# Recurrence on one core: where 48 modulation steps are issued, and two heads' blocks side by side

## The chip, the cores and the metric

The kernel runs on one core of a Trainium2 chip, in one launch. The metric is the device time of that core in microseconds (us). The engines named below are PE (TensorE, the matrix multiplies), DVE (VectorE), ACT (ScalarE), POOL (GpSimd) and SP (SyncE, which here only issues transfers). Each engine runs its own list of instructions in the order in which they stand there. Before the change three runs took 1282.65, 1286.14 and 1279.99 us, with a median of 1282.65 us.

## The reference

A trunk of two layers works on 512 positions of width 1024. Layer 0 is a gated linear recurrence (8 heads of 128) with a SwiGLU feed-forward (FFN, inner width 2816). From its result one K and one V are projected. Layer 1 is a banded attention over them (16 heads of 64), with its own FFN. Every sub-layer normalises, then scales and shifts by vectors that come from a conditioning vector `c`:

```python
c_act = jax.nn.silu(c)
for layer in range(DEPTH):
    mod = c_act @ mod_w[layer] + mod_b[layer]
    sh1, sc1, g1, sh2, sc2, g2 = jnp.split(mod, N_MOD, axis=-1)
    u = modulate(rms_norm(h, norm_mix[layer]), sh1, sc1)
    mix = hgrn2_mixer(...) if layer < N_A_LAYERS else chunk_band_attention(...)
    h = h + g1[:, None, :] * mix
    u = modulate(rms_norm(h, norm_ffn[layer]), sh2, sc2)
    h = h + g2[:, None, :] * swiglu(u, ffn_w_in[layer], ffn_w_out[layer])
    if layer == N_A_LAYERS - 1:
        k_pad, v_pad = shared_kv(h, c_act, kv_norm, kv_mod_w, kv_mod_b, kv_w)
return rms_norm(h, final_norm)
```

`shared_kv` has a shift and a scale of its own from `c`. So there are 14 modulation vectors of 1024 entries. In the recurrence, position t takes from position s of the same head the value `q_t * decay(s..t) * k_s`, and `decay` is a product of the forget gates between them.

## The kernel before

**Modulation steps.** Two of the 14 vectors are made at the start; the other 12 come from `mod_vector` (line 308 on), eight steps for each vector. One step loads 128 rows of 1024 weights (512 KB) into a tile `mw` by SP (line 313) and multiplies it by the row `crow` with a sum along the row, on DVE (line 315). `mw` has two buffers, so a third load waits until the first step is done. After eight steps one small addition (line 317) gives the vector. `mod_vectors` chains vectors, and each `next(side, None)` asks for one more step. A step is held back behind the instruction that `state["mods_after"]` names when the step is asked for (line 314).

**Order.** Apart from the first part (written in a manual order), a scheduler sorts the instructions of each engine. It may take a step that the program asks for late and put it earlier, as far as its data and line 314 let it. The order that it made is fixed when the program runs: an instruction that waits holds up all that stand behind it on its engine. Weights are loaded by SP into three buffers (`raw`), about two pieces ahead (`load`), and split by ACT (line 123, high part) and DVE (line 128, low part) one piece ahead (`fetch`).

**Recurrence.** `core(p, ...)` works on heads 2p and 2p+1 (e = 0, 1), for p = 0 to 3. It goes through block lengths: single positions up to 16 (tile names `fine`), then 32, 64, 128 and 256 (names `l`). At each length small matrix products give the blocks between neighbouring halves, and `advance` multiplies q and k on DVE (lines 732 and 733) by decay totals (line 724), on which the next length waits. Between its stages `push` runs projections ("filler": names `av`, `zf`, `q`, `g`) so that PE has work, and asks for modulation steps at certain positions. Later stages are `o` (line 827), the norm over a head (`oms` on DVE, `ors` on POOL, `oe` on DVE), and the transposes `ot` (line 850).

**FFN of layer 0.** Input products: 4 output tiles of the plain kind, then 18 of a kind with seven products of half size (`fast_tiles`, tile `f_r`, lines 531 to 533), whose weights DVE must combine and split first. Then the output products (`f_o`, lines 183 to 185): tiles 0 and 1 together, then tiles 2 to 7, each in three pieces of the inner width. `residual` (line 329) adds a tile to `h[n]`. `ffn` asks for steps there: 3 after each of 3 pieces for tiles 0 and 1, then 2, 2 and 1 for each tile, and `drain(side)` at its end asks for what is left.

**K and V.** `early_pair` (names `e_k`, line 277 on) computes the first two K tiles from `us2` while the norm is still being made: `n_ss` (mean square), `n_dg` (line 253, DVE) and `n_rb` (broadcast). Then eight inputs `ukvh`, `ukvl` (lines 301 and 305) feed V's projection (`bv`), and eight inputs `uqh`, `uql` feed the queries (`bq`). DVE makes the low halves of all of them.

Of the kernel before, what the change touches and what calls it, by code (L numbers as in the profile page):

```python
# [13 lines left out]
AF = mybir.ActivationFunctionType  # L14
ALU = mybir.AluOpType

P = 128
# [3 lines left out]
NB = S // P  # L21
# [45 lines left out]
def trunk(ctx: ExitStack, tc: tile.TileContext, d, out):  # L67
    nc = tc.nc
    T, A, V, G = nc.tensor, nc.scalar, nc.vector, nc.gpsimd
# [65 lines left out]
    state = {"loaded": 0, "split": 0, "used": 0}  # L135
# [352 lines left out]
    def fast_tiles(fp, nm, slot, activated, kept, side):  # L488

        H = S // 2  # L490
        ops = {}

        def halves(key, raw, n_):
            wh = wp.tile([P, n_, 4, P], F32R, tag="wh", name=f"{key}_h")
            wl = wp.tile([P, n_, 4, P], F32R, tag="wl", name=f"{key}_l")
            A.activation(wh, raw, AF.Copy)  # L496
            V.tensor_sub(wl, raw, wh)  # L497
            return [(wh[:, i], wl[:, i]) for i in range(n_)]

        def prepare(n):  # L500

            m = f"{nm}_{n}"
            c1 = take((nm, n, "c1")).rearrange("p (o j) c -> p o j c", o=2)
            c2 = take((nm, n, "c2")).rearrange("p (o j) c -> p o j c", o=2)
            x1 = fp.tile([P, 2, 4, P], F32, tag="x1", name=f"{m}_x1")
            x2 = fp.tile([P, 2, 4, P], F32, tag="x2", name=f"{m}_x2")
            b11, b21, b22, b12 = c1[:, 0], c1[:, 1], c2[:, 0], c2[:, 1]
            t2, t1, t3, t4 = x1[:, 0], x1[:, 1], x2[:, 0], x2[:, 1]
            ops[n, 1], ops[n, 2] = halves(f"{m}_w1", c1, 2)
            V.tensor_sub(t1, b12, b11)  # L510
            V.tensor_sub(t2, b22, t1)
            yield
            ops[n, 6], ops[n, 5] = halves(f"{m}_w2", x1, 2)
            V.tensor_sub(t3, b22, b12)
            V.tensor_sub(t4, b21, t2)
            yield
            ops[n, 7], ops[n, 4] = halves(f"{m}_w3", x2, 2)
            yield
            ops[n, 3], = halves(f"{m}_w4", c2[:, 0:1], 1)
            yield  # L520

        def stream():
            for n in range(PLAIN, FT):
                yield from prepare(n)

        def product(n, i, ps, s, start, stop):
            wh, wl = ops.pop((n, i))
            for j in range(4):
                uh, ul = slot(j, s)
                f = start and j == 0  # L530
                T.matmul(ps, wh[:, j, :], uh, start=f, stop=False, skip_group_check=True)  # L531
                T.matmul(ps, wh[:, j, :], ul, start=False, stop=False, skip_group_check=True)  # L532
                T.matmul(ps, wl[:, j, :], uh, start=False, stop=stop and j == 3, skip_group_check=True)  # L533

        chunks = stream()
        done = {"n": 0}

        def ahead(upto):
            while done["n"] < upto and next(chunks, chunks) is not chunks:
                done["n"] += 1  # L540

        AHEAD = 2
        for i, n in enumerate(range(PLAIN, FT)):
            at = activated(n)
            r1, r2, r3 = (bank(f"{nm}_r{q}_{n}")[:, 0:H] for q in (1, 2, 3))
            pu = sm.tile([P, 2, H], F32, tag="ut", name=f"{nm}_pu{n}", bufs=2)
            qu = sm.tile([P, 2, H], F32, tag="et", name=f"{nm}_qu{n}", bufs=2)
            p1, u2, p5, u3 = pu[:, 0, :], pu[:, 1, :], qu[:, 0, :], qu[:, 1, :]
            row1, row2 = at[:, H:S], at[:, 0:H]

            ahead(4 * i + 1 + AHEAD)
            product(n, 1, r1, 1, True, True)
            A.activation(p1, r1, AF.Copy)  # L553
            product(n, 5, r2, 4, True, True)
            A.activation(p5, r2, AF.Copy)
            ahead(4 * i + 2 + AHEAD)
            product(n, 6, r1, 5, False, True)
            A.activation(u2, r1, AF.Copy)
            product(n, 2, r3, 3, True, True)
            V.tensor_add(p1, r3, p1)  # L560
            A.activation(p1, p1, AF.Silu)
            ahead(4 * i + 3 + AHEAD)
            product(n, 7, r1, 6, False, True)
            A.activation(u3, r1, AF.Copy)
            ahead(4 * i + 4 + AHEAD)
            product(n, 3, r2, 7, False, True)
            V.tensor_add(row2, u3, p5)
            V.tensor_add(row1, r2, u2)
            V.tensor_mul(row1, row1, p1)
            product(n, 4, r1, 2, False, True)  # L570
            A.activation(p5, r1, AF.Silu)
            V.tensor_mul(row2, row2, p5)
            kept(n, at)
            if i % 2:
                next(side, None)
        fetch(state["used"] - 1, 1)


    mods = ctx.enter_context(ExitStack())
# [89 lines left out]
    def mod_vectors(names):  # L669
        return _chain.from_iterable(mod_vector(vectors.index(v), C_MB + 8 * vectors.index(v), mod[v]) for v in names)  # L670
# [41 lines left out]
    def core(p, qq, ks, f):  # L712
# [24 lines left out]
        ps = bank(f"fine{p}_0")  # L737
        pv = ps.rearrange("p (n l c) -> p n l c", l=2, c=32)
        for b in range(NB):
            for e in range(2):  # L740
                for j in range(4):
                    c = b * P + 32 * j
# [20 lines left out]
        adv = ad.rearrange("p e b c -> p (e b) c")  # L763

        ps = bank(f"l32_{p}")
        pv = ps[:, 0:256].rearrange("p (n c) -> p n c", c=32)
        for e in range(2):
            for m in range(8):
                r = 64 * (m % 2)
                T.matmul(pv[r:r + 32, e * NB + m // 2, :], ks[:, e, 64 * m:64 * m + 32],  # L770
                         qp[:, e, 64 * m + 32:64 * m + 64], start=True, stop=True)
        advance(32, t)
        t = totals(32, t)
        for j in range(4):
            r = slice(32 * j, 32 * j + 32)
            A.activation(adv[r, :, r], af[r, :, :], AF.Copy)
        for r in (0, 64):
            A.activation(adv[r:r + 32, :, r + 32:r + 64], pv[r:r + 32], AF.Copy)
        yield

        ps = bank(f"l64_{p}")
        pv = ps.rearrange("p (n c) -> p n c", c=64)
        for e in range(2):
            for m in range(4):
                T.matmul(pv[0:64, e * NB + m, :], ks[:, e, P * m:P * m + 64],
                         qp[:, e, P * m + 64:P * m + P], start=True, stop=True)
        advance(64, t)
        t = totals(64, t)
        A.activation(adv[0:64, :, 64:P], pv[0:64], AF.Copy)
        yield  # L790

        ps = bank(f"l128_{p}")
# [126 lines left out]
            yield from output_gate(hd)  # L919

    late = []
    side = mod_vectors(("g1", "sc2", "sh2", "g2", "sck", "shk"))
    fill = filler()
    pos = 0

# [5 lines left out]
    def push(upto):  # L931
        nonlocal pos
        while pos < upto:
            if next(fill, fill) is fill:
                pos = 1 << 30
                return
            pos += 1
            if pos > 49 and pos % (7 if pos < 114 else 3) == 0:
                next(side, None)

    with tc.manual_schedule():
# [145 lines left out]
    else:  # L1087
        u = [modulated(up, "u", j, rb, a_f[:, j:j + 1], mod["sh2"][:, j:j + 1], "u1") for j in range(KT)]
        state["mods_after"] = state["modulated"]
    side = mod_vectors(("sc1b", "sh1b", "g1b", "sc2b", "sh2b", "g2b"))  # L1090
    acc = sm.tile([P, S], F32, tag="nacc", name="acc2", bufs=1)
    us = []
    a_kv = cst.tile([P, KT], F32, tag="a_kv", name="a_kv")
# [360 lines left out]
```

## Time and profile before

| what | value |
|---|---|
| median of three runs | 1282.65 us (1279.99 to 1286.14) |
| the profiled execution's own time | 1283.68 us |
| its span on the core, granted TensorE clock | 1281.5 us, 0.996 |
| PE busy, weight loads busy | 1255.6 us, 1070.2 us |
| DVE busy, ACT busy | 990.7 us, 637.7 us |
| modulation steps: loads, mean of the multiply | 96 of 512 KB, 1221 ns |
| HBM read | 171.96 MB |

All times in the profile are of one execution, counted from its span's start. The views used below are the page (shares of the whole), windows (busy time of each engine in a stretch; "x" is the number of instructions), the timeline (instructions in order of time: start, duration, engine, line, operation, tiles, count; in square brackets the idle time before it and what ended it), and the waits (who waited for whom). Ends of matrix products are modelled, so their starts are used. In the timeline of DVE one instruction's end laps over the next one's start, so a step's price is read from start to start.

### The profile page before, as it was taken

What the parts mean: (1) busy time and instruction counts of PE and PEld (TensorE: products, weight loads), DVE (VectorE), ACT (ScalarE), POOL (GpSimd) and SP (SyncE); (2) the same over time, 40 slices, a digit from 0 to 9 for tenths busy, and PEclk for the clock granted to TensorE, in tenths of its full rate; (3) what the DMA queues carried; (4) which work ended last, traced back from release to release, by engine and by line L of the source; (5) the groups of instructions that cost most, each with busy time, mean ns of one, the idle gap of its engine ahead of it and who ended that gap; (6) DMA issues with size and microseconds to landing.
All of it is one profiled execution on the core that took longest, in us unless ns stands there. A gap on an engine that the chain in (4) does not pass through costs nothing.

```text
span 1281.5 us, 21575 instructions
## 1 busy us (share of the span) xinstructions
PE 1255.6 (98%) x8544; PEld 1070.2 (84%) x8544; DVE 990.7 (77%) x1812; ACT 637.7 (50%) x1119; POOL 20.8 (2%) x28
## 2 busy tenths in 40 slices
PE   7999999999999999999999999999999999999996
PEld 6878778788899999978888766676889999998886
DVE  7998888946999999986359656776798888884324
ACT  4464436443655565642228456674465556563220
POOL 0000000000000000000000000000000000000000
PEclk9999999999999999999999999999999999999999
DMA  9456666522455655666342322211333333342321
GB/s 367 166 181 194 224 223 207 193 80 85 109 203 182 197 185 195 209 204 204 91 130 82 107 74 73 79 58 34 115 91 107 104 114 113 100 124 91 94 88 66
DMA packets 53333, 177.55 MB, mean 139 GB/s; under 512 B 6000, under 2 KB 9456, under 8 KB 53232
## 3 DMA queue, kind: packets, MB, share of 16 engines
q1 hardware_dynamic: 52656, 174.08, 41.3%
q0 software_dynamic: 576, 2.10, 1.0%
q8 instruction: 67, 1.10, 0.4%
q14 instruction: 34, 0.28, 0.1%
HBM read 171.96 MB, written 2.10 MB: 136 GB/s over the span
## 4 chain that ended last, share of the span: by engine, by line
PE 81%; DVE 12%; DMA 3%; issue 2%; ACT 1%; POOL 1%; SPq 0%; POOLq 0%; DVEq 0%; ACTq 0%
PE f_r L532 8%; PE f_r L533 8%; PE f_r L531 7%; PE f_o L185 6%; PE f_o L183 6%; PE f_o L184 6%; DVE mw L315 2%; DMA mw<-in_modw 2%; PE t L1183 2%; PE f L183 2%; PE f L184 2%; PE f L185 2%; PE s L1166 2%; DVE f_w_l L497 1%; PE bo L1197 1%
## 5 line engine op out<-in xcount | busy, mean ns | idle before, releaser
L532 PE MATMUL f_r<-f_l,f_w_h 128*128 128x256 f32 x1008 | 287.0, 285 | 0.0
L533 PE MATMUL f_r<-f_h,f_w_l 128*128 128x256 f32 x1008 | 282.1, 280 | 0.9 <-DVE f_w_l L497 0.8
L531 PE MATMUL f_r<-f_h,f_w_h 128*128 128x256 f32 x1008 | 280.7, 279 | 0.0
L533 PEld LDWEIGHTS f_r<-f_h,f_w_l 128*128 128x128 f32 x1008 | 189.0, 188 | 2.1 <-DVE f_w_l L497 1.9
L531 PEld LDWEIGHTS f_r<-f_h,f_w_h 128*128 128x128 f32 x1008 | 189.5, 188 | 0.3 <-ACT f_pu L553 0.2
L532 PEld LDWEIGHTS f_r<-f_l,f_w_h 128*128 128x128 f32 x1008 | 189.5, 188 | 0.1
L185 PE MATMUL f_o<-f_p,f_o_l 128*128 128x512 f32 (+1 forms) x374 | 141.6, 380 | 0.5 <-DVE f_o_l L128 0.5
L183 PE MATMUL f_o<-f_p,f_o_h 128*128 128x512 f32 (+1 forms) x374 | 141.9, 380 | 0.0
L184 PE MATMUL f_o<-f_p,f_o_h 128*128 128x512 f32 (+1 forms) x374 | 140.9, 377 | 0.2 <-DVE f_p L448 0.2
L315 DVE SCALAR_TENSOR_TENSOR mw<-mw,crow 128x1024 f32<-128x1024 f32 x96 | 116.8, 1221 | 17.5 <-DMA mw<-in_modw 17.3
L123 ACT ACTIVATE f_o_h<-r_f_o 128x1024 fp32r<-128x1024 f32 (+1 forms) x48 | 46.8, 987 | 137.8 <-PE f_o L184 116.6
L128 DVE TENSOR_TENSOR f_o_l<-r_f_o,f_o_h 128x1024 fp32r<-128x1024 f32 (+1 forms) x48 | 54.0, 1134 | 69.0 <-ACT f_o_h L123 62.4
L496 ACT ACTIVATE f_w_h<-f_x 128x1024 fp32r<-128x1024 f32 x72 | 76.5, 1062 | 49.3 <-PE f_r L532 40.6
L497 DVE TENSOR_TENSOR f_w_l<-f_x,f_w_h 128x1024 fp32r<-128x1024 f32 x72 | 88.0, 1223 | 5.7 <-ACT f_w_h L496 3.2
L496 ACT ACTIVATE f_w_h<-r_f_c 128x1024 fp32r<-128x1024 f32 x72 | 61.0, 847 | 49.0 <-PE f_r L532 47.4
L185 PEld LDWEIGHTS f_o<-f_p,f_o_l 128*128 128x128 f32 x374 | 70.1, 188 | 15.8 <-DVE f_o_l L128 1.9
L184 PEld LDWEIGHTS f_o<-f_p,f_o_h 128*128 128x128 f32 x374 | 70.2, 188 | 14.5 <-DVE f_p L448 0.7
L183 PEld LDWEIGHTS f_o<-f_p,f_o_h 128*128 128x128 f32 x374 | 70.3, 188 | 12.5
L497 DVE TENSOR_TENSOR f_w_l<-r_f_c,f_w_h 128x1024 fp32r<-128x1024 f32 x72 | 68.8, 955 | 10.1 <-ACT f_w_h L496 10.1
L1172 ACT ACTIVATE sb<-sb,st 128x128 f32<-128x128 f32 (+1 forms) x64 | 35.6, 557 | 41.5 <-DVE st L1171 41.3
L1169 DVE CUSTOM_DVE_ANT_0 sb<-s,wb 128x128 f32<-128x128 f32 (+1 forms) x64 | 31.0, 490 | 29.5 <-PE s L1166 29.2
L184 PE MATMUL f<-f_l,f_h 128*128 128x512 f32 x96 | 37.4, 396 | 0.0
(381 smaller groups left out, 2724.2 us busy)
## 6 DMA issues: line engine op xcount, KB each, us to landing
mw<-in_modw SPq DMA_DIRECT2D x96, 512.0 KB, 4.1
r_f_c<-in_ffn_in SPq DMA_DIRECT2D x72, 512.0 KB, 3.4
r_f_o<-in_ffn_out SPq DMA_DIRECT2D x32, 512.0 KB, 3.7
mrow<-in_modw SPq DMA_DIRECT2D x16, 512.0 KB, 8.7
r_f<-in_ffn_in SPq DMA_DIRECT2D x16, 512.0 KB, 3.3
r_f_o<-in_ffn_out SPq DMA_DIRECT2D x16, 384.0 KB, 3.3
r_av<-in_a_v SPq DMA_DIRECT2D x8, 512.0 KB, 3.7
r_g<-in_a_g SPq DMA_DIRECT2D x8, 512.0 KB, 4.5
```

The lines of the kernel that those rows point to most:

```text
L123: A.activation(wh, raw, AF.Copy)
L128: V.tensor_sub(wl, raw, wh)
L183: T.matmul(ps, wh[:, kt, :], uh, start=start, stop=False)
L184: T.matmul(ps, wh[:, kt, :], ul, start=False, stop=False)
L185: T.matmul(ps, wl[:, kt, :], uh, start=False, stop=stop)
L315: V.scalar_tensor_tensor(mw, mw, 1.0, crow, op0=ALU.mult, op1=ALU.mult, accum_out=raw[:, j:j + 1])
L496: A.activation(wh, raw, AF.Copy)
L497: V.tensor_sub(wl, raw, wh)
L531: T.matmul(ps, wh[:, j, :], uh, start=f, stop=False, skip_group_check=True)
L532: T.matmul(ps, wh[:, j, :], ul, start=False, stop=False, skip_group_check=True)
L533: T.matmul(ps, wl[:, j, :], uh, start=False, stop=stop and j == 3, skip_group_check=True)
L1172: A.activation(s[:, 0:n], s[:, 0:n], AF.Exp, bias=st[:, 1:2], accum_out=st[:, 2:3])
```

## The change

There are four edits. In the recurrence the list of vectors loses `sck` and `shk` (16 steps), so 32 steps are left there, and `push` asks for one every 5 positions instead of every 7 and then every 3. The 16 steps go to the head of the list for the first FFN, which now has 64. At the end of `fast_tiles`, `mods_after` is set to that stage's last multiplication, so steps asked for later stand behind the input products. In `core`, the blocks of lengths 32 and 64 of the two heads are put on different partitions of the same PSUM columns, and the loop alternates between the heads; the copies from there are made per head.

```diff
-            V.tensor_mul(row2, row2, p5)
+            last = V.tensor_mul(row2, row2, p5)
...
         fetch(state["used"] - 1, 1)
+        state["mods_after"] = last
...
-        pv = ps[:, 0:256].rearrange("p (n c) -> p n c", c=32)
-        for e in range(2):
-            for m in range(8):
-                r = 64 * (m % 2)
-                T.matmul(pv[r:r + 32, e * NB + m // 2, :], ks[:, e, 64 * m:64 * m + 32],
+
+        pv = ps[:, 0:128].rearrange("p (n c) -> p n c", c=32)
+        for m in range(8):
+            for e in range(2):
+                r = 64 * (m % 2) + 32 * e
+                T.matmul(pv[r:r + 32, m // 2, :], ks[:, e, 64 * m:64 * m + 32],
                          qp[:, e, 64 * m + 32:64 * m + 64], start=True, stop=True)
...
-        for r in (0, 64):
-            A.activation(adv[r:r + 32, :, r + 32:r + 64], pv[r:r + 32], AF.Copy)
+        for e in range(2):
+            for r in (0, 64):
+                A.activation(ad[r:r + 32, e, :, r + 32:r + 64], pv[r + 32 * e:r + 32 * e + 32], AF.Copy)
...
-        pv = ps.rearrange("p (n c) -> p n c", c=64)
-        for e in range(2):
-            for m in range(4):
-                T.matmul(pv[0:64, e * NB + m, :], ks[:, e, P * m:P * m + 64],
+        pv = ps[:, 0:256].rearrange("p (n c) -> p n c", c=64)
+        for m in range(4):
+            for e in range(2):
+                T.matmul(pv[64 * e:64 * e + 64, m, :], ks[:, e, P * m:P * m + 64],
                          qp[:, e, P * m + 64:P * m + P], start=True, stop=True)
...
-        A.activation(adv[0:64, :, 64:P], pv[0:64], AF.Copy)
+        for e in range(2):
+            A.activation(ad[0:64, e, :, 64:P], pv[64 * e:64 * e + 64], AF.Copy)
...
-    side = mod_vectors(("g1", "sc2", "sh2", "g2", "sck", "shk"))
+    side = mod_vectors(("g1", "sc2", "sh2", "g2"))
...
-            if pos > 49 and pos % (7 if pos < 114 else 3) == 0:
+            if pos > 49 and pos % 5 == 0:
...
-    side = mod_vectors(("sc1b", "sh1b", "g1b", "sc2b", "sh2b", "g2b"))
+    side = mod_vectors(("sck", "shk", "sc1b", "sh1b", "g1b", "sc2b", "sh2b", "g2b"))
```

The steps are numbered `mw<vector>_<step>` below: 2 to 5 are `g1`, `sc2`, `sh2`, `g2`; 13 and 12 are `sck` and `shk`; 7, 6, 8, 10, 9 and 11 are the six vectors of layer 1.

**In the recurrence**, on DVE, in the middle of head pair p = 2. Before, steps of `sck` stand between the multiplications of q and k:

```order
L317 TENSOR_TENSOR mod_g2_129<-mcol5_2235,cols_67 128x8
L315 SCALAR_TENSOR_TENSOR mw13_0_2440,mcol13_2439<-mw13_0_2440,crow_114 128x1024
L732 TENSOR_TENSOR qq2_1779<-qq2_1779,t2_8_2072 128x32x16
L733 TENSOR_TENSOR ks2_1781<-ks2_1781,t2_8_2072 128x32x16
L761 COPY_PREDICATED af2_1856<-masks_801,fine2_16_2087 128x256
L128 TENSOR_TENSOR q_7_l_2215<-r_q_7_2131,q_7_h_2214 128x1024
L732 TENSOR_TENSOR qq2_1779<-qq2_1779,t2_16_2122 128x16x32
L733 TENSOR_TENSOR ks2_1781<-ks2_1781,t2_16_2122 128x16x32
L315 SCALAR_TENSOR_TENSOR mw13_1_2503,mcol13_2439<-mw13_1_2503,crow_114 128x1024
L315 SCALAR_TENSOR_TENSOR mw13_2_2553,mcol13_2439<-mw13_2_2553,crow_114 128x1024
L732 TENSOR_TENSOR qq2_1779<-qq2_1779,t2_32_2166 128x8x64
```

With the change:

```order
L317 TENSOR_TENSOR mod_g2_129<-mcol5_2340,cols_67 128x8
L733 TENSOR_TENSOR qq2_1794<-qq2_1794,t2_8_2075 128x32x16
L734 TENSOR_TENSOR ks2_1796<-ks2_1796,t2_8_2075 128x32x16
L762 COPY_PREDICATED af2_1867<-masks_801,fine2_16_2090 128x256
L128 TENSOR_TENSOR q_7_l_2218<-r_q_7_2134,q_7_h_2217 128x1024
L733 TENSOR_TENSOR qq2_1794<-qq2_1794,t2_16_2125 128x16x32
L734 TENSOR_TENSOR ks2_1796<-ks2_1796,t2_16_2125 128x16x32
L733 TENSOR_TENSOR qq2_1794<-qq2_1794,t2_32_2169 128x8x64
```

The addition that ends the 32nd step is DVE's row 253 in both programs. Behind it the 16 steps of `sck` and `shk` are gone; ahead of it the steps stand within a few rows of their old places.

**In the output products of the first FFN**, on DVE, from the residual of tile 3 on. Before, no step stands there:

```order
L329 SCALAR_TENSOR_TENSOR h3_74<-f0_o3_0_6350,mod_g2_129,h3_74 128x512
L128 TENSOR_TENSOR f0_o_4_2_l_6500<-r_f0_o_4_2_6461,f0_o_4_2_h_6499 128x768
L230 TENSOR_TENSOR acc2_3376<-acc2_3376,n2_sq3_0_6453 128x512
L265 SCALAR_TENSOR_TENSOR us2l3_6457<-h3_74,a_kv_3377,us2h3_6456 128x512
L128 TENSOR_TENSOR f0_o_5_0_l_6536<-r_f0_o_5_0_6497,f0_o_5_0_h_6535 128x1024
L128 TENSOR_TENSOR f0_o_5_1_l_6574<-r_f0_o_5_1_6533,f0_o_5_1_h_6573 128x1024
L329 SCALAR_TENSOR_TENSOR h4_75<-f0_o4_0_6460,mod_g2_129,h4_75 128x512
```

With the change six steps stand between the residuals of tiles 3 and 4:

```order
L329 SCALAR_TENSOR_TENSOR h3_74<-f0_o3_0_6310,mod_g2_129,h3_74 128x512
L315 SCALAR_TENSOR_TENSOR mw6_4_6451,mcol6_6345<-mw6_4_6451,crow_114 128x1024
L230 TENSOR_TENSOR acc2_3336<-acc2_3336,n2_sq3_0_6413 128x512
L265 SCALAR_TENSOR_TENSOR us2l3_6417<-h3_74,a_kv_3337,us2h3_6416 128x512
L128 TENSOR_TENSOR f0_o_4_2_l_6460<-r_f0_o_4_2_6421,f0_o_4_2_h_6459 128x768
L315 SCALAR_TENSOR_TENSOR mw6_5_6454,mcol6_6345<-mw6_5_6454,crow_114 128x1024
L315 SCALAR_TENSOR_TENSOR mw6_6_6487,mcol6_6345<-mw6_6_6487,crow_114 128x1024
L128 TENSOR_TENSOR f0_o_5_0_l_6496<-r_f0_o_5_0_6457,f0_o_5_0_h_6495 128x1024
L315 SCALAR_TENSOR_TENSOR mw6_7_6490,mcol6_6345<-mw6_7_6490,crow_114 128x1024
L317 TENSOR_TENSOR mod_sh1b_130<-mcol6_6345,cols_67 128x8
L315 SCALAR_TENSOR_TENSOR mw8_0_6519,mcol8_6518<-mw8_0_6519,crow_114 128x1024
L128 TENSOR_TENSOR f0_o_5_1_l_6534<-r_f0_o_5_1_6493,f0_o_5_1_h_6533 128x1024
```

Each tile from 2 to 7 has five or six steps like this, with the splits of the weights (line 128) between them. Of the 64 steps of this FFN, 9 stand among its input products (33 did before), 43 between their end and the residual of tile 7, and 12 behind it.

**At the start of V's projection**, on DVE. Before, the split `bv_0_2_l` of V's third piece of weights stands between the inputs 3 and 4:

```order
L301 SCALAR_TENSOR_TENSOR ukv_t4_7035<-h4_75,a_kv_3377,n2_rb0_6973 128x512
L301 SCALAR_TENSOR_TENSOR ukv_t5_7041<-h5_76,a_kv_3377,n2_rb0_6973 128x512
L128 TENSOR_TENSOR bv_0_2_l_7157<-r_bv_0_2_7124,bv_0_2_h_7156 128x1024
L305 SCALAR_TENSOR_TENSOR ukvl4_7038<-ukv_t4_7035,mod_shk_136,ukvh4_7037 128x512
L305 SCALAR_TENSOR_TENSOR ukvl5_7044<-ukv_t5_7041,mod_shk_136,ukvh5_7043 128x512
```

With the change it stands behind the last step and input 7:

```order
L315 SCALAR_TENSOR_TENSOR mw11_5_6908,mcol11_6892<-mw11_5_6908,crow_114 128x1024
L305 SCALAR_TENSOR_TENSOR ukvl5_7056<-ukv_t5_7053,mod_shk_136,ukvh5_7055 128x512
L301 SCALAR_TENSOR_TENSOR ukv_t6_7059<-h6_77,a_kv_3337,n2_rb0_6985 128x512
L301 SCALAR_TENSOR_TENSOR ukv_t7_7065<-h7_78,a_kv_3337,n2_rb0_6985 128x512
L315 SCALAR_TENSOR_TENSOR mw11_6_6911,mcol11_6892<-mw11_6_6911,crow_114 128x1024
L305 SCALAR_TENSOR_TENSOR ukvl6_7062<-ukv_t6_7059,mod_shk_136,ukvh6_7061 128x512
L315 SCALAR_TENSOR_TENSOR mw11_7_6914,mcol11_6892<-mw11_7_6914,crow_114 128x1024
L305 SCALAR_TENSOR_TENSOR ukvl7_7068<-ukv_t7_7065,mod_shk_136,ukvh7_7067 128x512
L317 TENSOR_TENSOR mod_g2b_135<-mcol11_6892,cols_67 128x8
L301 SCALAR_TENSOR_TENSOR uq_t0_7074<-h0_71,a_q_6920,n2_rb0_6985 128x512
L301 SCALAR_TENSOR_TENSOR uq_t1_7080<-h1_72,a_q_6920,n2_rb0_6985 128x512
L128 TENSOR_TENSOR bv_0_2_l_7169<-r_bv_0_2_7136,bv_0_2_h_7168 128x1024
```

The 12 steps behind tile 7's residual stand among the norm and the inputs of K and V. On SP the loads of these steps stand between the weight loads `r_f0_o`, `r_k` and `r_bv`, in the same order.

## The prediction

> **What bounds the kernel now.** I read the page first, then busy time by stretch, then the waits of PE, then the timeline of DVE where the change puts work. From the page:
>
> ```profile
> span 1281.5 us, 21575 instructions
> PE 1255.6 (98%) x8544; PEld 1070.2 (84%) x8544; DVE 990.7 (77%) x1812; ACT 637.7 (50%) x1119; POOL 20.8 (2%) x28
> PE 81%; DVE 12%; DMA 3%; issue 2%; ACT 1%; POOL 1%; SPq 0%; POOLq 0%; DVEq 0%; ACTq 0%
> ```
>
> PE holds 81% of the chain that ended last, so a change gains by shortening PE's work or the few stalls in it, and loses by adding stalls. The windows show where PE waits and who has room there. Columns: stretch and length, then busy us and instructions of PE, its weight loads, DVE, ACT and POOL, then clock, DMA share, GB/s.
>
> ```profile
> 123.00:195.00 72.00, 67.43 (x961) 53.96 (x960) 63.36 (x110) 31.17 (x58) 2.28 (x3) 1.00 0.66 217
> 195.00:262.00 67.00, 65.07 (x714) 53.78 (x713) 55.89 (x97) 35.71 (x77) 1.99 (x2) 1.00 0.58 191
> 358.00:451.00 93.00, 92.15 (x769) 91.43 (x768) 91.82 (x153) 53.39 (x91) 0.00 (x0) 1.00 0.59 193
> 451.00:541.00 90.00, 89.92 (x748) 89.13 (x748) 89.67 (x149) 53.60 (x93) 0.00 (x0) 1.00 0.58 193
> 560.00:600.00 40.00, 39.53 (x173) 32.15 (x172) 29.43 (x44) 12.19 (x15) 0.00 (x0) 1.00 0.74 247
> 600.00:663.00 63.00, 63.00 (x277) 51.66 (x277) 27.16 (x42) 17.35 (x21) 0.19 (x3) 1.00 0.32 101
> 663.00:707.00 44.00, 44.00 (x205) 36.59 (x204) 38.34 (x56) 30.22 (x45) 1.24 (x4) 1.00 0.32 100
> ```
>
> PE is idle 4.57 us of the recurrence from 123 to 195 and 1.93 us from 195 to 262. In the FFN's input products (358 to 541) it is nearly full, and so is DVE: 181.5 of 183 us. In its output products (600 to 663) DVE is busy 27 of 63 us: that is the room the change aims at. From 663 to 707, at K and V, DVE is busy 38.3 of 44 us: little room. PE's waits in the recurrence (engine, line, who ended it, us in total, times, longest; the first two rows 120 to 195, the last one 195 to 262):
>
> ```profile
> PE ot L850 <- DVE oe L841: 1.6, 1, 1.6
> PE fine L757 <- DVE ks L733: 0.9, 2, 0.7
> PE fine L757 <- DVE ks L733: 1.5, 2, 0.8
> ```
>
> **Part 1, the recurrence loses 16 steps.** They stood behind row 253 of DVE, that is from about 195 on. They free 16 starts of 1.14 us on DVE (price below) and their loads on SP. I give the change the whole 1.9 us that PE idles from 195 to 262. From 123 to 195 the same steps stand nearly where they stood, so I count nothing there, although the spacing in the program is new; one step more ahead of `oms` of pair 0 could even cost a step's load. Bounds: 0 and 4.57 + 1.93 = 6.5 us.
>
> **Part 2, two heads side by side.** The nearest rows, PE's timeline:
>
> ```profile
> 148.61 0.70 PE L770 MATMUL l<-qq,ks 128*32 128x32 f32 x32
> 149.24 0.50 PE L183 MATMUL q<-u0h,q_h 128*128 128x512 f32 x1
> ...
> 151.50 1.15 PE L785 MATMUL l<-qq,ks 128*64 128x64 f32 x16
> 152.57 0.50 PE L183 MATMUL zf<-u0h,zf_h 128*128 128x512 f32 x1
> ...
> 90.07 0.76 PE L757 MATMUL fine<-qq,ks 128*32 128x32 f32 x64
> 90.77 0.50 PE L206 MATMUL av<-av_h,u0h 128*128 128x512 f32 x1
> ```
>
> The 32 products of length 32 take 0.63 us now, on two column groups. `fine` runs the same size on four groups: 64 in 0.70 us, so 32 in about 0.38 (half, and a little tail, an estimate): 0.25 us less. The 16 of length 64 take 1.07 us on one group; on two I take 0.6, 0.45 less. That is 0.7 us for a pair, 2.8 us for four. Where PE next waits for DVE the gain is swallowed (pairs 1 and 2 have the waits above), so I take 2.0; bounds 0 and 2.8. The Trainium skill, TensorEngine Tiling (Array Packing), Instruction Overhead, speaks against the smaller half: a product with few columns costs as much as one of about 60, so 32 columns should not be tiled. By it the 0.25 us would be 0 and the part would be worth 1.8 at most; the 64 products of `fine` in 0.70 us are against it. ACT gets three more copies for each pair, none longer than the one of line 778 (32 rows of 256, min/median/max in ns):
>
> ```profile
> L778 ACT ACTIVATE ad<-l x8: 373/375/377, 103.4 to 248.1; 32x256 f32<-32x256 f32 x8
> ```
>
> ACT idles over half of 123 to 195, which hides them. Without that cover 3 * 0.375 us for four pairs would be 4.5 us.
>
> **Part 3, the input products of the first FFN lose 24 steps.** The same stage in both layers, tile `f_r`; the second layer has no steps:
>
> ```profile
> 358.00:538.00 180.00, 179.06 (x1493) 177.65 (x1492) 14.70 (x35) 33.42 (x89) 1.00 0.58 190
> 968.00:1148.00 180.00, 179.72 (x1512) 179.51 (x1510) 15.28 (x36) 33.57 (x89) 1.00 0.33 105
> ```
>
> In 180 us the first is 19 products behind; at 180 / 1512 = 0.119 us that is 2.3 us. Nine steps stay at the stage's start, so I take 2.0 back; bounds 0 and 2.8.
>
> Gains together: 1.9 + 2.0 + 2.0 = 5.9 us; bounds 0 and 12.1.
>
> **Part 4, 55 steps behind the input products.** Before there were 15 of them. This is where I expect the time to go. The stretch of before in which steps come closest, on DVE (its other rows left out):
>
> ```profile
> 543.28 8.52 DVE L448 TENSOR_TENSOR f_p<-f_ar,f_p 128x512 fp32r<-128x512 f32 x14
> ...
> 576.69 1.22 DVE L315 SCALAR_TENSOR_TENSOR mw<-mw,crow 128x1024 f32<-128x1024 f32 x1
> ...
> 577.83 1.23 DVE L315 SCALAR_TENSOR_TENSOR mw<-mw,crow 128x1024 f32<-128x1024 f32 x1
> ...
> 581.26 1.23 DVE L315 SCALAR_TENSOR_TENSOR mw<-mw,crow 128x1024 f32<-128x1024 f32 x1 [1.05 <-DMA mw<-in_modw]
> ...
> 583.60 1.23 DVE L315 SCALAR_TENSOR_TENSOR mw<-mw,crow 128x1024 f32<-128x1024 f32 x1 [1.11 <-DMA mw<-in_modw]
> ...
> 596.45 1.23 DVE L315 SCALAR_TENSOR_TENSOR mw<-mw,crow 128x1024 f32<-128x1024 f32 x1 [1.40 <-DMA mw<-in_modw]
> ```
>
> Two steps back to back start 1.14 us apart, the price on DVE. But DVE waits for the load: from 576.69 to 596.45 there are eight steps (three rows left out), 19.76 / 7 = 2.83 us each, because two buffers go round: load, multiply, load again. The first of the 55 starts when six splits of 0.61 us (8.52 / 14) behind the last multiplication are done, at 543.28 + 3.7 = 547. At 2.83 us the 55th starts at 547 + 54 * 2.83 = 699.8 and ends its place at 701. Weight loads `r_f_o` and `r_k` are queued on SP behind loads that wait for a buffer, and splits (line 128), residuals and inputs on DVE behind steps that wait for a load; PE waits for these. By 662.7, when tile 7's residual is due, 43 steps should be through; at this pace the 43rd starts at 665.9. So the output products lose little. What is late next is K and V:
>
> ```profile
> 662.73 0.75 DVE L329 SCALAR_TENSOR_TENSOR h<-f_o,mod_g,h 128x512 f32<-128x512 f32 x1 [1.98 <-PE f_o L185]
> ...
> 669.07 0.88 DVE L253 TENSOR_SCALAR n_dg<-ident,n_rs 128x128 f32<-128x128 f32 x4 [2.46 <-POOL n_rs L244]
> ...
> 687.13 1.42 DVE L305 SCALAR_TENSOR_TENSOR ukvl<-ukv_t,mod_shk,ukvh 128x512 fp32r<-128x512 f32 x2
> 688.46 1.40 DVE L301 SCALAR_TENSOR_TENSOR uq_t<-h,a_q,n_rb 128x512 f32<-128x512 f32 x2
> 689.78 1.22 DVE L128 TENSOR_TENSOR bq_l<-r_bq,bq_h 128x1024 fp32r<-128x1024 f32 x1
> ```
>
> ```profile
> 675.70 0.48 PE L206 MATMUL bv<-bv_h,ukvh 128*128 128x512 f32 x1
> ...
> 697.59 0.40 PE L183 MATMUL bq<-uqh,bq_h 128*128 128x512 f32 x1
> ...
> 703.10 0.39 PE L183 MATMUL bq<-uqh,bq_h 128*128 128x512 f32 x1
> ```
>
> Behind the 55th step stand the low half of input 7 (0.66 us from start to start), two `uq_t` (1.32) and the split `bv_0_2_l` (1.13): ready at 704.1. PE needs it for the second half of V's 96 products (21.89 us, 0.228 each). It has then 43 of them left (in the new order four go ahead) and 23 of the first query tile's 24, 66 * 0.228 = 15.0 us: done at 719.1, where before it was 703.1. **Loss 16.0 us.**
>
> Bounds of this part. Below: no step ever waits for its load. Then DVE's 12 late steps remain: 13.7 us on a stretch that ended with input 7 at 688.46. Two fit into the 2.46 us before `n_dg` (2.3), two splits have moved behind (2.3): 688.46 + 13.7 - 4.6 = 697.6, and by the same tail 715.2, a loss of 12.1 us. Above: a saturated DMA. The pace of before over 560 to 600, gaps included, is 12 steps from 562.06 to 596.45:
>
> ```profile
> 562.06 1.23 DVE L315 SCALAR_TENSOR_TENSOR mw<-mw,crow 128x1024 f32<-128x1024 f32 x1 [2.86 <-DMA mw<-in_modw]
> 580.00:590.00 10.00, 10.00 (x46) 8.19 (x45) 6.96 (x11) 3.13 (x4) 0.00 (x0) 1.00 0.91 301
> ```
>
> that is 34.4 / 11 = 3.13 us, 16.2 us later at the 55th: a loss of 32. The window row shows why it could be: 0.91 of the DMA at 301 GB/s, while six steps of 0.524 MB and a tile's weights (two pieces of 512 KB, one of 384) are 4.6 MB in the 15 us of a tile's 66 products, 304 GB/s. I take 2.83, the pace with both transfers in flight.
>
> **Sum.** 1283.7 - 5.9 + 16.0 = 1293.8 us against the profiled execution's own 1283.68, which is 1.0 above the median of the three runs. Against the median: 1292.8, so **1293 us**.
>
> **Rivals.**
>
> *The loads keep up.* Only the 12 late steps cost, 12.1 us: 1283.7 - 5.9 + 12.1 - 1.0 = 1289 against the median. For it: the first load of a pair (577.95 on SP's timeline) is used 3.3 us later. Against it: of the eight steps above five waited for their load. The Trainium skill, DMA: Bandwidth & Descriptors, Anatomy of one DMA, gives about 2.0 us plus the bytes at 436 GB/s for a transfer issued from GpSimd, 3.2 us as estimate for 512 KB; by that two buffers make 2.2 us a step, and this rival would hold. The median of these loads here is 4.1.
>
> ```profile
> 577.95 1.47 SPq L313 DMA_DIRECT2D mw<-in_modw  x2
> DMA to landing us min/median/max: 3.1/4.1/6.0
> ```
>
> *The DMA saturates.* Steps at 3.13 us; weight splits between them are late too, so PE stalls already in the output products, and the loss is between 16 and 32, say 28: 1283.7 - 5.9 + 28 - 1.0 = 1305.
>
> *The recurrence recovers everything*, the one that ends on the other side. All of PE's idle time there is DVE's doing and goes (6.5), with 2.8 and 2.8 from parts 2 and 3: 12.1 gained. With a loss of 12.1 at K and V that cancels: 1283, not slower; from there each microsecond that PE saves by work of its own while `bv_0_2_l` is late makes it faster. For it: PE's waits above are mostly on DVE. Against it: the steps of the first three quarters keep their places, and of PE's work only one product of `bq` was moved ahead.
>
> *The change doesn't spread what it says.* On DVE the steps up to row 253 stand where they stood; that is already in part 1. It would cost the 1.9 us at most.
>
> **How the numbers follow.** Forecast 0.53 (1288 to 1300 by itself), loads keep up 0.24, DMA saturates 0.15, recovery 0.08. The range reaches from full recovery to the saturated case: 1282 to 1306. A measurement of this kernel can tell about 0.5% (6.4 us) from no change, so slower means over 1289. Of the forecast 0.45 lies above that and 0.08 below; of the second case half; the third all above: 0.45 + 0.12 + 0.15 = 0.72. Within 0.5%: 0.08 + 0.12 and a part of the last case, 0.22. Faster: 0.06, the rest of that case.
>
> **What would show it.** Right: DVE idle before `mw` "<-DMA" in most of 55 rows from 547 on, about 2.8 us apart, the last at about 700 less the gains; PE waiting on DVE at `e_k`, `n_ss` and `bv` between 655 and 715, by 10 to 20 us; `f_r` of both layers at one pace within 0.7 us; the blocks `l` of lengths 32 and 64 (lines 772 and 788 now) at about 0.4 and 0.6 us a pair. Wrong: steps 2.2 us apart with no idle time before them; PE without waits at `bv`; PE's idle time from 123 to 195 gone as well.

## The result and the profile after

The changed kernel takes 1304.56 us (median of 4 runs, 1302.58 to 1307.2) against 1283.28 us for the kernel before (median of 4, 1279.99 to 1286.14). The ratio is 1.0168, with a 95% interval of 1.0137 to 1.0199. It is slower, as forecast, and inside the range, but by 21 us where the forecast had about 10.

The profiled execution of the changed kernel took 1304.2 us, 20.5 more than the one of before. From its page:

```profile
span 1302.2 us, 21603 instructions
PE 1258.2 (97%) x8544; PEld 1068.9 (82%) x8544; DVE 1000.7 (77%) x1812; ACT 639.7 (49%) x1131; POOL 22.1 (2%) x28
```

PE executes the same 8544 products; the 20.7 us by which the span grew are waits and a slower clock, as the rows below show. The same windows as before (stretch and length, then busy us and instructions of PE, its weight loads, DVE, ACT and POOL, then clock, DMA share, GB/s) show where:

```profile
123.00:195.00 72.00, 66.49 (x960) 53.11 (x960) 62.41 (x110) 31.48 (x61) 3.25 (x3) 1.00 0.66 214
195.00:262.00 67.00, 66.39 (x726) 54.38 (x724) 39.07 (x62) 37.05 (x90) 3.58 (x3) 1.00 0.20 64
560.00:600.00 40.00, 40.00 (x176) 32.82 (x175) 29.80 (x47) 11.76 (x15) 0.00 (x0) 1.00 0.78 267
600.00:663.00 63.00, 58.14 (x253) 47.06 (x251) 49.09 (x85) 16.25 (x20) 0.00 (x0) 0.99 0.84 270
663.00:707.00 44.00, 29.25 (x118) 21.59 (x119) 39.43 (x68) 16.34 (x23) 2.37 (x5) 0.85 0.63 207
```

Up to 262 PE is about as full as it was (66.5 and 66.4 us against 67.4 and 65.1). From 663 to 707 it ran 118 products where it ran 205, and the granted clock is 0.85 where it was 1.00. Followed through the program, with the start of the same instruction in both traces:

| first instruction of its kind | before | changed | difference |
|---|---|---|---|
| transposes `ot` of the last pair (recurrence done) | 266.0 | 262.3 | -3.7 |
| output products of the first FFN | 540.3 | 535.3 | -5.1 |
| first product of K (`e_k`) | 662.5 | 656.6 | -6.0 |
| K done (`n_b`) | 675.3 | 679.6 | +4.2 |
| first query tile done | 703.1 | 722.9 | +19.8 |
| second FFN (`e_f`) | 921.0 | 941.2 | +20.1 |

So the gains came to 6.0 us (forecast 5.9), and the stretch at K and V lost 6.0 + 19.8 = 25.8 us (forecast 16.0). PE's waits from 655 to 725 (engine, line, who ended it, us in total, times, longest):

```profile
PE bq L183 <- ACT uqh L304: 9.1, 1, 9.1
PE e_k L185 <- DVE k_l L128: 6.1, 2, 5.8
PE bv L208 <- DVE ukvl L305: 2.7, 3, 1.7
PE n_ss L235 <- DVE acc L230: 1.2, 1, 1.2
```

The forecast named `e_k`, `n_ss` and `bv`, and 10 to 20 us in all; with the 0.4 us of a row left out here the waits are 19.5 us. The longest stands at `bq`: it is the one query product that PE's new order puts ahead of V's second half, and it ends when that half's split `bv_0_2_l` is nearly done (705.82 against 706.13). The releasers stand on DVE, or on ACT behind DVE, in line behind modulation steps. DVE's timeline, first and last step and what follows it (other rows left out):

```profile
541.89 1.22 DVE L315 SCALAR_TENSOR_TENSOR mw<-mw,crow 128x1024 f32<-128x1024 f32 x1
...
701.79 1.23 DVE L315 SCALAR_TENSOR_TENSOR mw<-mw,crow 128x1024 f32<-128x1024 f32 x1 [0.47 <-DMA mw<-in_modw]
...
703.68 1.40 DVE L301 SCALAR_TENSOR_TENSOR uq_t<-h,a_q,n_rb 128x512 f32<-128x512 f32 x2
705.00 1.22 DVE L128 TENSOR_TENSOR bv_l<-r_bv,bv_h 128x1024 fp32r<-128x1024 f32 x1
```

The 55 steps begin 5.1 us earlier than forecast, which is the gain by then, and end 2.0 us later (54 steps in 159.9 us, 2.96 us each instead of 2.83). The view of the tile `mw` from 541 to 702 (the steps, DVE's idle time before them in us and times, and the loads from issue to landing):

```profile
L315 DVE SCALAR_TENSOR_TENSOR mw<-mw,crow x55: 1215/1224/1228, 541.9 to 701.8; 128x1024 f32<-128x1024 f32 x55
...
  DMA mw<-in_modw: 22.2, 26
...
DMA to landing us min/median/max: 3.1/4.3/6.9
```

A buffer goes round in 2 * 2.96 = 5.92 us: 4.3 for the load (the median), 1.22 for the multiplication, and a remaining 0.4. Of that, 0.1 passes until SP issues the next load; in the rest the load has landed and DVE is still at something else. That is why DVE waits before 26 of the steps only, and not before most of the 55.

PE's timeline at the two long waits shows a second effect, which no part of the forecast had:

```profile
658.00 0.40 PE L184 MATMUL e_k<-us2l,k_h 128*128 128x512 f32 x1
664.24 0.79 PE L185 MATMUL e_k<-us2h,k_l 128*128 128x512 f32 x1 [5.85 <-DVE k_l L128]
664.83 0.63 PE L183 MATMUL e_k<-us2h,k_h 128*128 128x512 f32 x1
...
668.13 0.40 PE L185 MATMUL e_k<-us2h,k_l 128*128 128x512 f32 x1
...
705.82 0.80 PE L183 MATMUL bq<-uqh,bq_h 128*128 128x512 f32 x1 [9.10 <-ACT uqh L304]
...
708.98 0.40 PE L207 MATMUL bv<-bv_l,ukvh 128*128 128x512 f32 x1
```

After each wait the products take 0.63 us instead of 0.40 and start about 0.43 us apart instead of 0.228, until 668.1 and 709.0. From 705.82 to 708.98 seven starts take 3.16 us instead of 1.60: 1.6 us more. The windows cut at these points show the granted clock (columns as above):

```profile
655.00:661.20 6.20, 3.14 (x13) 1.94 (x11) 4.99 (x13) 1.06 (x1) 0.00 (x0) 1.00 0.83 258
661.20:668.00 6.80, 3.76 (x9) 2.99 (x10) 6.39 (x14) 0.00 (x0) 0.00 (x0) 0.50 0.76 239
668.00:698.70 30.70, 24.31 (x108) 17.67 (x106) 26.98 (x47) 11.14 (x15) 1.97 (x1) 1.00 0.67 224
698.70:709.00 10.30, 3.18 (x8) 2.47 (x9) 9.83 (x17) 7.15 (x12) 0.40 (x4) 0.50 0.49 146
```

It falls to half for 6.8 and for 10.3 us.

The gains, too, have their rows. PE's timeline in the recurrence of the changed kernel, then one window for the products `f_r` of each layer:

```profile
137.32 0.75 PE L758 MATMUL fine<-qq,ks 128*32 128x32 f32 x64 [3.54 <-DVE ks L734]
...
150.22 0.46 PE L772 MATMUL l<-qq,ks 128*32 128x32 f32 x32
150.61 0.50 PE L183 MATMUL q<-u0h,q_h 128*128 128x512 f32 x1
...
152.87 0.69 PE L788 MATMUL l<-qq,ks 128*64 128x64 f32 x16
153.49 0.50 PE L183 MATMUL zf<-u0h,zf_h 128*128 128x512 f32 x1
```

```profile
354.30:534.30 180.00, 179.50 (x1504) 1.00 0.39 129
988.10:1168.10 180.00, 179.76 (x1512) 1.00 0.33 105
```

The blocks of lengths 32 and 64 now take 0.39 and 0.62 us. The input products are 8 products behind the second layer's in 180 us, where they were 19 behind: 11 * 0.119 = 1.3 us won. That leaves the two layers 0.95 us apart, a little more than the 0.7 that the forecast asked for.

### The profile page after: what moved, and what is told of

Same layout as the page of the kernel before. It is cut to its first block, busy times and chain, and to the rows that moved or that the text cites. A ratio compares the mean times of both kernels' runs of the same rounds, so it can differ in the third digit from the quotient of the medians.

```text
span 1302.2 us, 21603 instructions
## 1 busy us (share of the span) xinstructions
PE 1258.2 (97%) x8544; PEld 1068.9 (82%) x8544; DVE 1000.7 (77%) x1812; ACT 639.7 (49%) x1131; POOL 22.1 (2%) x28
## 4 chain that ended last, share of the span: by engine, by line
PE 60%; issue 27%; DVE 7%; DMA 3%; ACT 2%; POOL 0%; SPq 0%; POOLq 0%; DVEq 0%; ACTq 0%
PE f_r L532 5%; PE f_r L533 5%; PE f_r L531 4%; PE f_o L184 3%; PE f_o L183 3%; PE f_o L185 3%; DMA mw<-in_modw 3%; PE t L1187 2%; PE s L1170 2%; DVE mw L315 1%; PE bo L1201 1%; PE bq L183 1%; PE f L183 1%; PE f L184 1%; DVE mrow L619 1%
## 5 line engine op out<-in xcount | busy, mean ns | idle before, releaser
L315 DVE SCALAR_TENSOR_TENSOR mw<-mw,crow 128x1024 f32<-128x1024 f32 x96 | 116.6, 1220 | 29.5 <-DMA mw<-in_modw 29.2
```

What stands on the lines that cost most here:

```text
L315: V.scalar_tensor_tensor(mw, mw, 1.0, crow, op0=ALU.mult, op1=ALU.mult, accum_out=raw[:, j:j + 1])
```

## The experiments

Every run is compared with the kernel before on the same chip (median 1283.9 for the first four, 1284.4 for the others). "Theory 1" is the forecast's: the 55 steps go at the pace of their loads and end too late for K and V.

### 1. The heads side by side, alone

Edit to the kernel before: only the two blocks of part 2.

```diff
-        pv = ps[:, 0:256].rearrange("p (n c) -> p n c", c=32)
+        pv = ps[:, 0:128].rearrange("p (n c) -> p n c", c=32)
...
-                r = 64 * (m % 2)
+                r = 64 * (m % 2) + 32 * e
```

> The kernel before with part 2 of the change alone: two heads' blocks of lengths 32 and 64 side by side; all 48 steps of the recurrence and the 33 and 15 of the first FFN stay. Forecast (part 2): the two blocks shrink from 0.63 and 1.07 us to about 0.38 and 0.6 us a pair, and 2.0 us reach the end (0 to 2.8): about 1281. In the changed kernel the first transpose `ot` of the last pair came 3.7 us earlier than before; if part 2 makes most of that, it comes about 2 to 2.8 us earlier here, and the 16 steps taken out of the recurrence are worth the other 1 to 2 us. Rival: the gain is swallowed by PE's next wait on DVE, `ot` no earlier than 0.5 us, time as before, and all 3.7 us belong to the steps.

Measured: 1281.51 us, ratio 0.9984 (0.9974 to 0.9994), 2.1 us less by ratio (0.8 to 3.3). In the trace PE is 2.3 us further by the end of the recurrence, counted from its first product `zf` at 78 us. The forecast of 2.0 holds, and the rival in which PE's next wait swallows it falls.

### 2. Three buffers for the modulation rows

```diff
-            mw = mp.tile([P, D], F32, tag="mraw", name=f"mw{i}_{j}", bufs=2)
+            mw = mp.tile([P, D], F32, tag="mraw", name=f"mw{i}_{j}", bufs=3)
...
-            room = [("sp0", 1), ("sp1", 1)] + ...
+            room = [("sp0", 1)] + [("sp1", 1)] * layer + ...
```

> The changed kernel with three buffers for the rows of the modulation weights in place of two; 4 KB of room for the third come from one place for the splits of the hidden activations of the first FFN (one place fewer, one activation tile kept elsewhere). Theory 1 (the load sets the pace): two buffers give one step each (4.3 us landing + 1.22 us multiplication + some 0.3 us) / 2 = 2.9 us, as seen (2.96); three give a third, 1.9 us, unless the DMA saturates; the 55th step then starts between 542 + 54 * 1.94 = 647 and, if 304 GB/s is all the DMA gives (93 of it to the FFN's weights, 211 left, 2.48 us a step), 542 + 134 = 676. The loss at K and V, 26 us in the changed kernel, falls to between 0 and 13 us: time 1277 to 1291, best guess 1282, and no wait of PE over 3 us at K and V. Theory 2 (the steps' own time on DVE at K and V, whatever their loads): the loss stays over 12 us wherever steps are left there. Theory 3 (DMA already saturated with two): the pace stays at 2.9 us, landing times grow from 4.3 to over 6 us, and the time stays at about 1304.

Measured: 1293.28 us, ratio 1.0077 (1.0062 to 1.0092). The tile `mw` from 541 to 703, one window, and PE's waits from 655 to 725:

```profile
L315 DVE SCALAR_TENSOR_TENSOR mw<-mw,crow x55: 1215/1221/1228, 542.5 to 672.3; 128x1024 f32<-128x1024 f32 x55
...
DMA to landing us min/median/max: 3.1/4.7/6.8
```

```profile
545.00:655.00 110.00, 109.83 (x481) 89.78 (x480) 97.45 (x155) 34.21 (x43) 0.00 (x0) 1.00 0.89 304
```

```profile
PE bv L206 <- ACT ukvh L304: 4.6, 1, 4.6
PE n_ss L235 <- DVE acc L230: 3.1, 1, 3.1
```

The pace rises to 129.8 / 54 = 2.40 us a step, so two buffers were the limit and not the DMA; with three the DMA, at 0.89 and 304 GB/s, is near the rate at which the forecast put saturation, and DVE waits for a load before 14 of the 55 steps only. The last step starts 29.5 us earlier than in the changed kernel. Yet the time is above the expected 1277 to 1291. What was missed: the scheduler has put all 55 steps ahead of `n_dg` now, and `n_dg`, which belongs to the input of every later product, starts at 673.8, 10.0 us late against before less the 5.3 us gained by then. V begins 11.2 us late, and its first 13 products, with the clock at 0.50, take 2.7 us more. When the stream ends and what stands behind it in DVE's row decide together.

### 3. No hold behind the last multiplication

```diff
         fetch(state["used"] - 1, 1)
-        state["mods_after"] = last
```

> The changed kernel without the line that holds the steps of the first FFN behind its last multiplication: 32 steps in the recurrence and the heads side by side stay, but the scheduler puts 29 steps among the input products and 35 behind them, none at K and V. Theory 1: the 35 run from 542 to 542 + 34 * 2.96 = 643, before K and V's inputs are due at 657; no loss there, no clock below 1.00. Then all of the 26 us go, the 3.7 us of the recurrence stay, and the input products are within 1 us of before: about 1279. Rival: the slow stream also delays weights and residuals of the output products while it runs, 5 us or more before 655: over 1284.

Measured: 1281.34 us, ratio 0.9981 (0.9972 to 0.999). DVE's steps from 541 on in that run:

```profile
L315 DVE SCALAR_TENSOR_TENSOR mw<-mw,crow x31: 1212/1225/1228, 547.4 to 638.2; 128x1024 f32<-128x1024 f32 x31
```

The last one starts 63.6 us sooner, PE has no wait from 541 to 725, and the whole loss at K and V is gone; PE stands 4.9 us ahead there in the trace, and 4.4 at the end. So the whole loss comes from steps held too late, and the hold costs more than the steps did among the input products.

### 4. Sixteen steps back in the recurrence, with the hold

```diff
-    side = mod_vectors(("g1", "sc2", "sh2", "g2"))
+    side = mod_vectors(("g1", "sc2", "sh2", "g2", "sck", "shk"))
...
-            if pos > 49 and pos % 5 == 0:
+            if pos > 49 and pos % (7 if pos < 114 else 3) == 0:
...
-    side = mod_vectors(("sck", "shk", "sc1b", "sh1b", "g1b", "sc2b", "sh2b", "g2b"))
+    side = mod_vectors(("sc1b", "sh1b", "g1b", "sc2b", "sh2b", "g2b"))
```

> The changed kernel with the 16 steps (two vectors) and the old spacing back in the recurrence: 48 steps there, 9 at the start of the first FFN, 39 behind its input products, heads side by side. Theory 1: 39 steps from 542 on at 2.96 us end at 542 + 38 * 2.96 = 654.5, just before K and V's inputs are due: the loss of 26 us falls to 0 to 2. Gains left: part 2 (2 to 2.8) and part 3 (1.4 measured in the changed kernel). About 1279. It also tells parts 1 and 2 apart: `ot` of the last pair is earlier than before by part 2 alone. Rival (a few steps late cost much, since PE's pause lowers its clock): over 1285.

Measured: 1285.92 us, ratio 1.0015 (1.0001 to 1.0029): the expected 1279 was missed, and the rival held. The steps end as expected, but that is not soon enough. DVE's timeline, and then PE's:

```profile
654.84 1.22 DVE L315 SCALAR_TENSOR_TENSOR mw<-mw,crow 128x1024 f32<-128x1024 f32 x1
...
660.64 1.22 DVE L128 TENSOR_TENSOR k_l<-r_k,k_h 128x1024 fp32r<-128x1024 f32 x1
```

```profile
658.36 0.39 PE L184 MATMUL e_k<-us2l,k_h 128*128 128x512 f32 x1
661.91 0.50 PE L185 MATMUL e_k<-us2h,k_l 128*128 128x512 f32 x1 [3.17 <-DVE k_l L128]
...
662.92 0.63 PE L185 MATMUL e_k<-us2h,k_l 128*128 128x512 f32 x1
```

Behind the last two steps stand K's partial sums and the split `k_l`, so PE waits 3.2 us, and then eight products at half the clock cost 1.6 more. The stage goes from 5.1 us ahead to level: 5.1 us, for a split that was 3.2 us late: less than three of DVE's 1.15-us steps.

### 5. The pause filled

Edit to the kernel of run 4: extra products whose result is not used.

```diff
+                        spare = bank("spare")
+                        for _ in range(12):
+                            T.matmul(spare, wh[:, 0, :], uh, start=True, stop=True)
```

> The kernel of the run with sixteen steps back in the recurrence, with 12 extra products of 512 columns (0.228 us each, 2.7 us together, result unused, into a bank of their own) put on PE just ahead of the product of K that waited 3.2 us there. It leaves the wait and its cause alone and only keeps PE at work in it. In that run the stage of K lost 5.1 us, of which by the trace 3.35 us were the wait and about 1.6 us the next eight products at 0.427 us each, under a granted clock of 0.75 and 0.91 in the two 5-us slices. Theory 1 (the pause itself brings the lower clock): no product of K slower than 0.23 us, clock 1.00 throughout, the stage loses 3.3 to 3.7 us, time about 1.6 us shorter than that run's. Rival (the clock falls for another reason, a load on the chip at this place): the eight slow products stay and the time is the same or, by the extra products, up to 2.7 us longer.

Measured: 1283.57 us, ratio 0.9993 (0.9983 to 1.0003), against 1.0015 for run 4. PE's timeline and the window behind it:

```profile
656.54 2.92 PE L284 MATMUL spare<-us2h,k_h 128*128 128x512 f32 x12
659.85 0.50 PE L285 MATMUL e_k<-us2h,k_l 128*128 128x512 f32 x1 [0.39 <-DVE k_l L128]
660.19 0.40 PE L183 MATMUL e_k<-us2h,k_h 128*128 128x512 f32 x1
660.42 0.39 PE L184 MATMUL e_k<-us2l,k_h 128*128 128x512 f32 x1
```

```profile
659.40:662.80 3.40, 3.01 (x14) 2.36 (x13) 3.37 (x5) 0.72 (x1) 0.00 (x0) 1.00 0.57 183
```

No product behind the pause is slow and the clock stays at 1.00, so it was the pause that lowered it. That is one trace, but the other executions agree: the mean granted clock of ten was 0.992 in run 4 and is 0.995 here, where the kernel before has 0.994. The stage loses 4.0 us instead of 5.1 (3.3 to 3.7 expected). The intervals of the two times just overlap, so the saving of time, some 1 to 3 us, rests on the trace more than on them.

### 6. Sixteen steps back, three buffers

Edit: runs 2 and 4 together.

> The kernel with sixteen steps back in the recurrence, with three buffers for the modulation rows (and the one place fewer in the first FFN, as in the run with three buffers). The same 39 steps behind the input products, now at the 2.40 us a step measured with three buffers: they end at 542.5 + 38 * 2.40 = 634, some 20 us sooner, 20 us ahead of K's inputs. Theory 1 (it counts when the stream of steps ends, against K's inputs due at about 655): no wait of PE at K, the 5.1 us lost there are gone, gains of 2.5 (heads), 1.9 (input products) and 0.7 stay: about 1278.5, the fastest so far. Rival (the number of steps behind the input products costs DVE time wherever they end, or the fuller DMA delays the FFN's weights): PE waits over 1 us between 541 and 655, or 3 us at K again, and 1282 or more.

Measured: 1277.14 us, ratio 0.9943 (0.9927 to 0.996), faster than both kernels. The 39 steps and PE's only wait from 541 to 725:

```profile
L315 DVE SCALAR_TENSOR_TENSOR mw<-mw,crow x39: 1214/1222/1228, 539.9 to 634.8; 128x1024 f32<-128x1024 f32 x39
```

```profile
PE f_o L185 <- DVE f_o_l L128: 0.3, 1, 0.3
```

The same number of steps as in run 4, ending 20 us sooner, loses nothing at K. By ratio the time is some 9 us below run 4's, more than the 5.1 lost there: in this trace PE is also 5.8 us ahead at the end of the recurrence, where it was 2.7 in run 4. The third buffer serves the recurrence's steps too (DVE waits 2.2 us for their loads from 78 to 262, in run 4 6.1); how much of the lead comes from it and how much is chance is not shown.

### 7. No loads for the 55 steps

The steps multiply one resident tile and their loads are left out, so the last vectors are not those of the reference; only the time is read.

```diff
+            if len(state["kept"]) < 2:
                 mw = mp.tile([P, D], F32, tag="mraw", name=f"mw{i}_{j}", bufs=2)
                 nc.sync.dma_start(mw, d["modw"][i, j])
...
+            else:
+                mw, dst = state["kept"]
```

> The changed kernel with the loads of the 55 late steps left out: each multiplies the same resident tile, so the six vectors built from them are wrong and only the time is read. The scheduler, which sees no load, may place the steps somewhat earlier. Theory 1 (the load sets the pace of the stream): the 55 steps run at DVE's own pace wherever it has time, end before 655, no PE pause at K and V, the clock stays at 1.00, and the time is the one of before less the 6 us gained: about 1277. Rival (55 steps of 1.15 us, 63 us of DVE, are too many for the output products, whatever the loads): PE waits for splits or residuals between 541 and 655, or for K's inputs, and the time stays above 1288.

Measured: 1277.45 us (a single execution). The steps in that run:

```profile
L322 DVE SCALAR_TENSOR_TENSOR mw<-mw,crow x55: 1216/1219/1228, 541.2 to 651.0; 128x1024 f32<-128x1024 f32 x55
```

All 55 multiplications fit before K, at 2.03 us each, and PE waits nowhere from 541 to 725. So DVE's own time for the steps makes none of the loss by itself.

### 8. The control for the place taken away

Edit: run 2 without its third buffer.

> Control for the runs with three buffers: the changed kernel with the one place fewer in the first FFN and the activation tile kept elsewhere, but with two buffers as in the change. If that edit costs nothing by itself: the same stream at 2.9 to 3.0 us a step ending at about 702, PE's waits of 6 and 9 us at K and V, and about 1304. Rival (the place edit moves the FFN's splits): waits of PE between 541 and 560, and over 2 us away from 1304.

Measured: 1304.54 us (a single execution), the last step at 701.4, waits of 4.6 and 8.9 us at K and V. The edit that made room costs nothing that shows.

## Why the prediction was right in direction and wrong in size

**Part 1 (16 steps fewer in the recurrence, -1.9): not resolved, probably too large.** PE's idle time from 195 to 262 fell from 1.93 to 0.61 us, as thought. From 123 to 195 it rose from 4.57 to 5.51: a wait at `fine` of pair 1 went from 0.7 to 3.54 us. The price that the part mentioned and did not count is in it: the step ahead of `oms` of pair 0 waits 2.10 us for its load (at 121.26), and `oms` starts 1.0 us later than before; the loads of later steps add to it. In runs 3 and 7, with the same recurrence, the same wait is 1.9 us. Counted as in run 1, PE is ahead at the end of the recurrence by 2.3, 2.7 and 4.7 us with 48 steps and the heads side by side (runs 1, 4, 5), and by 3.5, 4.5, 4.8 and 3.4 with 32 (the changed kernel, runs 3, 7, 8). The means differ by 0.9 us, less than traces of the same recurrence do among themselves, so the steps may be worth 1 us or nothing.

**Part 2 (heads side by side, -2.0): right.** 0.39 and 0.62 us against 0.38 and 0.6 estimated; 2.1 us by the times of run 1, 2.3 in its trace. By the Trainium skill, TensorEngine Tiling (Array Packing), Instruction Overhead, as the prediction read it, the 32-column half would gain nothing; the trace disagrees with that reading: 0.63 to 0.39 us for 32 products.

**Part 3 (24 steps fewer among the input products, -2.0): 1.4** by the table, 1.3 by the window. The 0.9 us that the output products gained on top were in no term. The gains' sum, 6.0 against 5.9, is partly luck: parts that were too large and a gain that was in none cancel.

**Part 4 (55 steps behind, +16.0): the mechanism right, the size wrong: 25.8.** For the pace, one row of SP's timeline of the kernel before counts (two loads, the first at 568.08 and the second ending 2.95 us later):

```profile
568.08 2.95 SPq L313 DMA_DIRECT2D mw<-in_modw  x2
```

The part's own steps, with what was measured:

- First step at 547 less the gains: 541.9, right.
- **The pace, 2.83 us a step: this term failed.** It was 2.96, which over 54 steps is 7.1 us. The 2.83 was read over eight steps, that is seven intervals, of which the first was no interval of the stream: the loads of the steps at 576.69 and 577.83 had been issued at 568.08 and 570.71 and had long landed, so these two stood 1.14 us apart. The other six intervals give (596.45 - 577.83) / 6 = 3.10 us. In the long stream landing and multiplication alone give (4.3 + 1.22) / 2 = 2.76, and the rest of the round adds 0.2 to each step. The pace with gaps, 3.13, stood in the prediction as the bound; the truth lies between.
- K starts 6.0 us sooner, the stream only 5.1: 0.9 us more to wait.
- From `bv_0_2_l` ready to the first query tile done: 706.1 to 722.9, 16.8 us instead of 15.0. Of these 1.8 us the half clock behind the 9.1-us wait is 1.6. The first slow stretch, behind the wait at K, seems to cost nothing of its own: soon behind it, at `n_ss`, PE waits for DVE again, for 1.2 us.

16.0 + 7.1 + 0.9 + 1.8 = 25.8.

**The rivals.** "The loads keep up" falls: landing takes 4.3 us at the median, and without the loads (run 7) the loss is gone. In the eight steps of the prediction the median was 4.3 as well; the 4.1 quoted there is that of all 96 loads. The estimate of 3.2 us from the Trainium skill, DMA: Bandwidth & Descriptors, Anatomy of one DMA, is met by the fastest loads alone (3.1); it is for transfers issued from GpSimd, and SP issues these. "The DMA saturates" came nearest in time, 1305, for another reason than its own: its 3.13 us a step and PE's waits in the output products are not there, and run 2 moves more bytes a second: 304 GB/s from 545 to 655, where the changed kernel has 260 from 541 to 655. "The recurrence recovers everything" falls with the wait of 3.54 us. That the change does not do what it says falls with the steps' places.

**What stays open.** How much of the 21 us the lower clock has in the changed kernel itself is read from the spacing of its products; the pause was filled only in the kernel of run 4. Why a load takes 4.3 us at the median where the fastest takes 3.1 was not tried. Why the recurrence differs by 2 us between profiles was not followed.

## What to carry to other kernels

A stream of loads through two buffers went here at (landing + use + what else its engine does) / 2 = (4.3 + 1.22 + 0.4) / 2. A third buffer did not give two thirds of that, 1.97, but 2.40 us a step: landing grew to 4.7, and DVE alone took 2.03 without loads (run 7). The thing to work out is when the stream ends, against what stands behind it on that engine. Take the pace from the longest stretch there is, gaps included, and start it at a step that waits for its load. A small overrun can cost more than itself, when a pause of PE is followed by slow products, as in run 4; here one more buffer, and sixteen steps fewer behind the input products, turned 21 us of loss into 7 of gain.

## What was not expected of the hardware

The granted clock of PE falls to half in stretches of 3.4 us and multiples of it: 6.8 and 10.3 us in the changed kernel, 3.4 in run 4. PE's next products then start 0.43 us apart instead of 0.228. The Trainium skill, TensorE: Matmul & The Clock Gate, Part 1, has this as a window of about 3.4 us that runs freely, with half the clock after an idle one. On the length of the stretches the traces agree; on the pause that it takes they are less regular: one of 3.54 us (before 137.3 in the changed kernel) left the clock at 1.00, while one of 3.17 us (run 4) lowered it. In front of the same product `fine` one of 1.89 us in run 3 left it alone, and one of 1.90 us in run 7 did not:

```profile
136.50:139.90 3.40, 3.40 (x9) 2.72 (x9) 3.40 (x8) 0.00 (x0) 0.00 (x0) 0.50 0.62 206
```

Where a pause falls against the window seems to count as much as its length; that is an inference from these pauses and was not tried by itself.
